# The feed-forward down projection as seven half-size products, with weight sums made by accumulating DMAs

## The chip, the core and the metric

The kernel runs on one core of a Trainium2 chip. The metric is the device time of one execution in microseconds, as the median over runs. Five engines work side by side, each through its own instructions in order: TensorE (PE in the profile; its weight loads are PEld), VectorE (DVE), ScalarE (ACT), GpSimd (POOL) and SyncE (SP, which issues most DMAs). Accumulators of TensorE lie in PSUM, everything else on the chip in SBUF.

## What is computed

A stack of mixing layers over 512 tokens of 1024 features: a first block (sparse attention and gated linear attention), a gated feed-forward layer, then four further attention layers. All is float32. Only the feed-forward layer is changed:

```
h = rmsnorm(x, norm_ffn)
g = silu(h @ w_ffn_gate) * (h @ w_ffn_up)      # 512 x 2816
x = x + g @ w_ffn_down                         # 2816 x 1024
x = rmsnorm(x, norm_final)
```

## The kernel before

**Precision.** A float32 matrix is kept as two halves of a faster format: the high part is made by ScalarE (line 214) and the low part by VectorE (line 215). A product takes three matmuls, high by high, low by high and high by low (`mm3`, lines 273 to 276). A weight piece is a raw tile `wr` (pool of 3, loaded by SP through `wload`), and its halves `wh` and `wl` (pool of 6). Ah and Al are the halves of the activations.

**Feed-forward.** The 2816 hidden features are 22 chunks of 128. They are computed in pairs of chunks: `pair` makes the gate product of a pair by `halves_product` (already seven products of halves, matmuls of 256 columns, with weight sums made on VectorE), the up product plainly (`proj_feat`, 512 columns), then tanh on ScalarE, sums and products on VectorE, and the split of the result into the tiles `hdh` and `hdl`. The first four chunks are computed plainly, and `half_sums` prepares token sums for the rest. The halves of silu are folded in as a factor 0.5 later.

**Down.** After 8, 8 and 6 chunks `down` multiplies what is there with the matching rows of w_ffn_down through `out_proj`: for each half of the 1024 columns and each of four row blocks of 128 tokens, n chunks times three matmuls of 512 columns into one PSUM tile of the pool `pj` (three tiles; `s` and `t` have two, `o` one). The epilogue adds it to the residual:

```
nc.vector.scalar_tensor_tensor(out=xv, in0=ps, scalar=0.5, in1=xv, op0=ALU.mult, op1=ALU.add)
```

In the last part the epilogue also takes squares (ScalarE), the norm (`rms_scale` on POOL, then line 1038 on VectorE with the row `gf`, which POOL loads by `broadcast_row`) and transposes the block for the next layer (`to_feat`, line 372).

**Order.** The instructions of each engine are put in order once, when the kernel is built, by a scheduler with its own estimate of durations. The chip follows that order: an engine that waits at one instruction holds back all behind it.

Of the kernel before, what the change touches and what calls it, by code (L numbers as in the profile page):

```python
# [10 lines left out]
F32 = mybir.dt.float32  # L11
# [7 lines left out]
S = 512  # L19
# [13 lines left out]
FF_PARTS = (8, 8, 6)  # L33
# [94 lines left out]
class Net:  # L128
# [99 lines left out]
    def wload(self, w, k0, kc, *ranges, pool=None):  # L228

        n = sum(r[1] for r in ranges)  # L230
        t = (self.wraw if pool is None else pool).tile([128, 1024], F32, name="wr")
# [654 lines left out]
    def half_sums(self, pool, room):  # L886

        nc = self.nc
        lo, hi, t0, t1 = slice(0, 4), slice(4, 8), slice(0, 256), slice(256, 512)
        q = lambda t, k, tok: t[:, k, tok]  # L890
        f11, f21, f12, f22 = (room.tile([128, 4, 256], F32, name=n) for n in ("f11", "f21", "f12", "f22"))
        for f, k, tok in ((f11, lo, t0), (f22, hi, t1), (f21, lo, t1), (f12, hi, t0)):
            nc.vector.tensor_tensor(out=f, in0=q(self.Ah, k, tok).bitcast(F32), in1=q(self.Al, k, tok).bitcast(F32), op=ALU.add)
        nc.vector.tensor_tensor(out=f22, in0=f21, in1=f22, op=ALU.add)
        nc.vector.tensor_tensor(out=f21, in0=f11, in1=f21, op=ALU.subtract)
        nc.vector.tensor_tensor(out=f11, in0=f22, in1=f11, op=ALU.subtract)
        nc.vector.tensor_tensor(out=f12, in0=f12, in1=f11, op=ALU.subtract)
        out = {"a11": (q(self.Ah, lo, t0), q(self.Al, lo, t0)), "a12": (q(self.Ah, hi, t0), q(self.Al, hi, t0)), "a22": (q(self.Ah, hi, t1), q(self.Al, hi, t1))}

        def splits():  # L900
            for n, src in (("s2", f11), ("s3", f21), ("s1", f22), ("s4", f12)):
                h, l = (pool.tile([128, 4, 256], F32R, name=n + u) for u in "hl")
                self.split_into(h, l, src)
                out[n] = (h, l)
            return out

        return splits

    def halves_product(self, pool, raws, sums, w, n0, out):
# [5 lines left out]
        v1 = self.wload(w, 0, KD, (n0 + 128, 128), pool=raws)  # L915
# [47 lines left out]
    def ffn(self):  # L963
        nc, a, tc = self.nc, self.a, self.tc
        with ExitStack() as c1:
            f1 = c1.enter_context(tc.tile_pool(name="f1", bufs=1))
            raws = c1.enter_context(tc.tile_pool(name="fr", bufs=1))
            most = max(FF_PARTS)
            hd = [f1.tile([128, most, S], F32R, name=n) for n in ("hdh", "hdl")]
            st = f1.tile([128, NB, 2], F32, name="fss")  # L970
            gf = f1.tile([128, D], F32, name="gf")
            self.broadcast_row(gf, a["norm_final"])
            wg, wu = a["w_ffn_gate"][0], a["w_ffn_up"][0]

            def hidden(m, s, u, tok=slice(0, S)):
# [4 lines left out]
            with tc.tile_pool(name="f0", bufs=1) as f0:  # L980
                for m in (0, 2):
                    wgs, wus = self.w_cols(wg, m * 128), self.w_cols(wu, m * 128)
                    for t in range(2):
                        halves = 1 if m or t else 2
                        for hf in range(halves):
# [5 lines left out]
                            s = f0.tile([128, S], F32, name="fg", bufs=2)[:, 0:n]  # L991
                            self.silu2(s, pg)
                            hidden(m + t, s, pu, tok)
                    if m == 0:
                        splits = self.half_sums(f1, f0)
                sums = splits()
            f2 = c1.enter_context(tc.tile_pool(name="f2", bufs=2))

            def pair(m, col):
# [466 lines left out]
```

## Time and profile before

| | |
|---|---|
| median of 3 runs | 1863.44 us (1862.99 to 1863.57) |
| the profiled execution | 1861.58 us |
| its span | 1859.8 us |
| TensorE busy | 1816.9 us, 98% |
| VectorE busy | 1216.1 us, 65% |
| ScalarE busy | 905.2 us, 49% |
| GpSimd busy | 155.6 us, 8% |

The span is the time from the first to the last instruction; the execution's own time has the start and end of the program in it too. Busy shares are of the span. Line numbers such as L1029 are those of the kernel printed above.

### The profile page before, as it was taken

The page shows a single profiled execution, that of the slowest core. Times are in us where ns is not written, and L with a number is a line of the kernel's source. Part 1 is how long each engine was busy: PE and PEld are TensorE (multiplying, and loading weights), DVE is VectorE, ACT ScalarE, POOL GpSimd, SP SyncE. Part 2 cuts the span into 40 slices and gives each one's busy share as a digit, 9 for nine tenths or more (in the row PEclk, how much of TensorE's full clock was granted, in tenths as well). Part 3 has the DMA queues.
Part 4 walks back from the last instruction along what each step waited for, and adds up shares of the span by engine and source line. Part 5 has one row for each costly group of instructions (what it writes and reads, how often), then busy time and mean ns, then how long its engine had stood idle before and what let it go on. Part 6 is the DMA issues. An engine that isn't in the chain of part 4 may idle for free.

```text
span 1859.8 us, 27291 instructions
## 1 busy us (share of the span) xinstructions
PE 1816.9 (98%) x10119; PEld 1494.7 (80%) x10119; DVE 1216.1 (65%) x3050; ACT 905.2 (49%) x2024; POOL 155.6 (8%) x213
## 2 busy tenths in 40 slices
PE   7999999999999999999999999999999999999997
PEld 6877787678888988889887798877888877988775
DVE  5554387754844664656878675576776666788866
ACT  4543236743432442445666444473565563366651
POOL 2211100000000000001000011242000000200001
PEclk9999999999999999999999999999999999999999
DMA  7222141042332442333221233211422222232111
GB/s 219 79 58 57 36 127 41 19 146 79 103 103 68 116 132 71 93 93 96 54 68 58 70 93 91 69 55 38 115 78 59 78 80 69 76 88 59 48 56 45
DMA packets 200751, 148.13 MB, mean 80 GB/s; under 512 B 8765, under 2 KB 178538, under 8 KB 200618
## 3 DMA queue, kind: packets, MB, share of 16 engines
q1 hardware_dynamic: 198826, 140.97, 26.5%
q0 software_dynamic: 1792, 5.42, 0.9%
q8 instruction: 79, 1.29, 0.3%
q14 instruction: 54, 0.44, 0.1%
HBM read 144.27 MB, written 2.10 MB: 79 GB/s over the span
## 4 chain that ended last, share of the span: by engine, by line
PE 91%; DVE 4%; ACT 2%; issue 2%; DMA 0%; POOL 0%; SPq 0%; POOLq 0%; DVEq 0%; ACTq 0%
PE pj L273 22%; PE pj L275 22%; PE pj L276 21%; PE o L350 4%; PE t L337 3%; PE pj L937 3%; PE s L937 1%; PE s L311 1%; PE o L273 1%; PE o L276 1%; PE s L275 1%; PE o L275 1%; PE s L273 1%; PE s L276 1%; DVE wl L215 1%
## 5 line engine op out<-in xcount | busy, mean ns | idle before, releaser
L214 ACT ACTIVATE wh<-wr 128x1024 fp32r<-128x1024 f32 (+9 forms) x406 | 294.6, 755 | 402.5 <-PE pj L275 158.0
L215 DVE TENSOR_TENSOR wl<-wr,wh 128x1024 fp32r<-128x1024 f32 (+9 forms) x406 | 338.3, 856 | 213.1 <-ACT wh L214 208.5
L273 PE MATMUL pj<-Ah,wh 128*128 128x512 f32 (+1 forms) x888 | 347.8, 392 | 2.2 <-DVE fg L288 0.9
L275 PE MATMUL pj<-Al,wh 128*128 128x512 f32 (+1 forms) x888 | 346.4, 390 | 0.2 <-DVE Al L215 0.2
L276 PE MATMUL pj<-Ah,wl 128*128 128x512 f32 (+1 forms) x888 | 345.6, 390 | 0.0
L273 PE MATMUL pj<-wh,Ah 128*128 128x512 f32 (+5 forms) x640 | 218.0, 341 | 4.7 <-ACT Ah L214 4.6
L275 PE MATMUL pj<-wl,Ah 128*128 128x512 f32 (+5 forms) x640 | 215.9, 337 | 0.0
L276 PE MATMUL pj<-wh,Al 128*128 128x512 f32 (+5 forms) x640 | 213.8, 338 | 2.1 <-DVE Al L215 2.0
L273 PEld LDWEIGHTS pj<-Ah,wh 128*128 128x128 f32 x888 | 167.3, 188 | 37.2 <-PE s L276 1.6
L276 PEld LDWEIGHTS pj<-Ah,wl 128*128 128x128 f32 x888 | 167.3, 188 | 35.0 <-issue 1.5
L275 PEld LDWEIGHTS pj<-Al,wh 128*128 128x128 f32 x888 | 167.3, 188 | 33.0 <-issue 0.8
L327 ACT ACTIVATE sp<-sp,nm 128x128 f32<-128x128 f32 (+3 forms) x256 | 142.9, 559 | 75.5 <-DVE nm L326 73.4
L205 ACT ACTIVATE pt<-t 128x512 f32<-128x512 f32 (+3 forms) x288 | 115.2, 445 | 105.9 <-PE t L337 66.6
L324 DVE CUSTOM_DVE_ANT_0 sp<-s,c_causal 128x128 f32<-128x128 f32 (+3 forms) x256 | 121.2, 487 | 56.5 <-PE s L276 23.5
L273 PEld LDWEIGHTS pj<-wh,Ah 128*128 128x128 f32 x640 | 120.6, 188 | 19.6 <-ACT Ah L214 7.3
L276 PEld LDWEIGHTS pj<-wh,Al 128*128 128x128 f32 x640 | 120.2, 188 | 14.1 <-DVE Al L215 3.1
L275 PEld LDWEIGHTS pj<-wl,Ah 128*128 128x128 f32 x640 | 120.7, 189 | 10.9 <-issue 0.2
L337 PE MATMUL t<-ident,sp 128*128 128x128 f32 x640 | 108.9, 278 | 5.1 <-ACT pt L205 5.0
L337 PEld LDWEIGHTS t<-ident,sp 128*128 128x128 f32 x640 | 77.3, 140 | 30.8 <-ACT pt L205 12.8
L331 DVE TENSOR_SCALAR sp<-sp,rc 128x128 f32<-128x128 f32 (+3 forms) x256 | 96.8, 383 | 5.0
L273 PE MATMUL pj<-wh,hdh 128*128 128x512 f32 x176 | 68.5, 390 | 0.3 <-DVE X L1029 0.3
L275 PE MATMUL pj<-wl,hdh 128*128 128x512 f32 x176 | 68.6, 390 | 0.0
(480 smaller groups left out, 3375.1 us busy)
## 6 DMA issues: line engine op xcount, KB each, us to landing
wr<-in_w_in_dram SPq DMA_DIRECT2D x34, 512.0 KB, 3.9
wr<-in_fox_w_in_dram SPq DMA_DIRECT2D x30, 512.0 KB, 4.1
wr<-in_w_ffn_gate_dram SPq DMA_DIRECT2D x22, 512.0 KB, 3.9
wr<-in_w_ffn_up_dram SPq DMA_DIRECT2D x22, 512.0 KB
wr<-in_w_ffn_down_dram SPq DMA_DIRECT2D x22, 512.0 KB, 3.8
wr<-in_swa_w_in_dram SPq DMA_DIRECT2D x20, 512.0 KB, 3.9
wr<-in_mla_w_in_dram SPq DMA_DIRECT2D x16, 512.0 KB, 3.9
wr<-in_mla_w_out_dram SPq DMA_DIRECT2D x16, 512.0 KB, 3.7
```

Source lines behind the costliest of these rows:

```text
L205: return self.nc.scalar.activation(out, in_, AF.Copy, scale=1.0 if scale is None else scale)
L214: self.nc.scalar.activation(h, src, AF.Copy)
L215: self.nc.vector.tensor_tensor(out=l, in0=src, in1=h.bitcast(F32), op=ALU.subtract)
L273: mm = self.nc.tensor.matmul(ps, lhsT=ah, rhs=bh, start=i == 0, stop=False)
L275: self.nc.tensor.matmul(ps, lhsT=ah, rhs=bl, start=False, stop=False)
L276: mm = self.nc.tensor.matmul(ps, lhsT=al, rhs=bh, start=False, stop=i == n - 1)
L324: nc.vector.tensor_tensor_reduce(out=v, in0=ps, in1=self.causal[:, S - n:S], scale=1.0, scalar=LOWEST, op0=ALU.add, op1=ALU.max, accum_out ...
L327: nc.scalar.activation(v, v, AF.Exp, bias=nm[:, g], accum_out=sm[:, g])
L331: nc.vector.tensor_scalar(v, v, rc[:, g], None, ALU.mult)
L337: nc.tensor.transpose(ps[:, (b - j) * 128:(b - j + 1) * 128], sp[:, POFF[b] + j * 128:POFF[b] + j * 128 + 128], self.ident)
L350: mm = self.nc.tensor.matmul(po[64 * i:64 * i + 64, j * 128:S], lhsT=value(j, i), rhs=pt[:, TOFF[j]:TOFF[j] + (NB - j) * 128], start=first ...
L937: nc.tensor.matmul(ps, lhsT=x, rhs=y, start=first and k == 0 and i == 0, stop=last and k == 3 and i == 2, skip_group_check=True)
```

## The change

The parts are now 6, 6, 6 and 4 chunks. With the chunks of a part taken as even and odd ones, tokens as two halves and columns as two halves, the down product is a two by two product of blocks, and it is made with seven products instead of eight. Each pair's hidden features are therefore combined into seven operands (`even`, `odd`), split into the tiles `hdh` and `hdl`, which now hold seven sets of 256 tokens. The weight sums are not made by an engine: a raw quarter of the weights is loaded into the tile x, split, and then the next quarter is added to it in place by a DMA that accumulates, issued by POOL; x receives three such additions, y one. Every product is added, with its sign, to the places of X that need it. The token sums (`half_sums`) are made in two pieces, and gf is loaded in the last part, into a tile that x used.

```diff
-FF_PARTS = (8, 8, 6)
+FF_PARTS = (6, 6, 6, 4)
...
+            def even(j, s, u):
                 nc.vector.tensor_tensor(out=s, in0=s, in1=u, op=ALU.mult)
-                self.split_into(hd[0][:, m, tok], hd[1][:, m, tok], s)
+                nc.vector.tensor_tensor(out=s[:, T1], in0=s[:, T0], in1=s[:, T1], op=ALU.subtract)
+                operands(j, 0, s)
+
+            def odd(j, pool, s, t, u):
+                nc.vector.tensor_tensor(out=t, in0=t, in1=u, op=ALU.mult)
+                e, f = (pool.tile([128, S], F32, name="fu", bufs=2) for _ in range(2))
+                nc.vector.scalar_tensor_tensor(out=e[:, T1], in0=s[:, T1], scalar=-1.0, in1=t[:, T1], op0=ALU.mult, op1=ALU.subtract)
+                nc.vector.tensor_tensor(out=e[:, T0], in0=e[:, T1], in1=s[:, T0], op=ALU.add)
+                operands(j, 4, e)
+                nc.vector.tensor_tensor(out=f[:, T0], in0=e[:, T1], in1=t[:, T0], op=ALU.add)
+                operands(j, 6, f[:, T0])
+                operands(j, 2, t)
...
+                def add(t, h, o):
+                    for v, (r, rc) in zip(t, pieces):
+                        nc.gpsimd.dma_start(v, quarter(r, rc, h, o), accum_op=ALU.add)
...
+                def update(ps, b, half, sign):
                     xv = self.X[:, b, half * 512:half * 512 + 512]
-                    nc.vector.scalar_tensor_tensor(out=xv, in0=ps, scalar=0.5, in1=xv, op0=ALU.mult, op1=ALU.add)
+                    nc.vector.scalar_tensor_tensor(out=xv, in0=ps, scalar=0.5 * sign, in1=xv, op0=ALU.mult, op1=ALU.add)
...
-                self.out_proj(a["w_ffn_down"][0], Split([(0, n, *hd)]), epilogue, kc=n, k0=k0)
+                x = raw(0, 0, raws.tile([128, 1536], F32, name="wr"))
+                w = weights(x)
+                pa = [self.pj(), self.pj()]
+                for i in range(2):
+                    product(pa[i], 0, w, i, first=True)
+                    update(pa[i], i, 0, 1)
+                add(x, 1, 0)
+                w = weights(x)
+                pc = [self.pss(), self.pss()]
+                for i in range(2):
+                    product(pc[i], 4, w, i, first=True)
+                    update(pc[i], 2 + i, 1, 1)
+                add(x, 1, 1)
+                w = weights(x)
+                for i in range(2):
+                    product(pa[i], 5, w, i)
+                    update(pa[i], i, 1, -1)
+                y = raw(1, 1)
+                w = weights(y)
+                for i in range(2):
+                    product(pc[i], 6, w, i, last=True)
+                    update(pc[i], i, 1, 1)
+                    squares(i, 1)
+                add(y, 1, 0)
+                w = weights(y)
+                for i in range(2):
+                    product(pa[i], 1, w, i)
+                    update(pa[i], 2 + i, 1, -1)
+                    squares(2 + i, 1)
+                w = weights(raw(0, 1))
+                add(x, 0, 1)
+                w4 = weights(x)
...
+                pb = [self.pst(), self.pst()]
+                for i in range(2):
+                    product(pb[i], 2, w, i, first=True, last=True)
+                    update(pb[i], i, 0, 1)
+                    squares(i, 0)
+                    norm(i)
+                for i in range(2):
+                    product(pa[i], 3, w4, i, last=True)
+                    update(pa[i], 2 + i, 0, 1)
+                    squares(2 + i, 0)
+                    norm(2 + i)
```

How the order of the instructions moves is shown at three places. A row has the line, the operation, the tile written and the tiles read, the shape, and the semaphores waited for: DMAHW is a DMA that SP issued, DMASW one that POOL issued, PE, DVE, Activation and Pool the engines.

ScalarE before, the last pair of the second part: fg_5948 and fg_5949 are its two gate results, fu its tanh, hdh its operands, the wh tiles weights.

```order
L214 ACTIVATE wh_6275<-wr_6273 128x1024 [waits DMAHW6_49,PE_49]
L214 ACTIVATE wh_6281<-wr_6279 128x1024 [waits DMAHW7_49,PE_49]
L205 ACTIVATE fg_5948<-pj_5974 128x256 [waits PE_49]
L1020 ACTIVATE fu_6109<-fg_5948 128x512 [waits Activation_49]
L1020 ACTIVATE fu_6112<-fg_5949 128x512 [waits DVE_49]
L214 ACTIVATE hdh_4339<-fg_5948 128x512 [waits DVE_49]
L214 ACTIVATE hdh_4339<-fg_5949 128x512 [waits DVE_49]
```

ScalarE after, the last pair of the second part: fg_5584 and fg_5585 are its gate results; wr_5791 is x of this down, wr_5886 and wr_5887 are y.

```order
L214 ACTIVATE wh_5858<-wr_5791 128x1024 [waits DMASW4_49,PE_49]
L205 ACTIVATE fg_5584<-pj_5610 128x256 [waits PE_49]
L1059 ACTIVATE fu_5745<-fg_5584 128x512 [waits DVE_49,Activation_49]
L1059 ACTIVATE fu_5748<-fg_5585 128x512 [waits DVE_49]
L214 ACTIVATE wh_5862<-wr_5791 128x512 [waits DMASW5_49]
L214 ACTIVATE wh_5890<-wr_5886 128x1024 [waits DMAHW7_49,PE_49]
L214 ACTIVATE wh_5894<-wr_5887 128x512 [waits DMAHW2_49,PE_49]
L214 ACTIVATE hdh_4339<-fg_5585 128x512 [waits DVE_49]
L214 ACTIVATE hdh_4339<-fg_5584 128x512 [waits DVE_49]
L214 ACTIVATE hdh_4339<-fu_5780 128x512 [waits DVE_49]
```

Where the operand splits followed the tanh directly, four weight splits now stand among them: one of an x sum ahead of the copy, and one of an x sum and two of y between tanh and operands.

TensorE after, the same pair: from the end of the last product of its gate (pj_5610, 17 rows above the first row here) on, 20 matmuls of the down need nothing of this pair; the last of them and what follows are shown.

```order
L1100 MATMUL pj_5803<-wh_5794,hdl_4340 128x512
L1100 MATMUL pj_5803<-wh_5794,hdh_4339 128x512
L1100 MATMUL pj_5803<-wl_5795,hdh_4339 128x512
L1100 MATMUL pj_5803<-wh_5794,hdl_4340 128x512
L1100 MATMUL pj_5802<-wh_5798,hdh_4339 128x512 [waits Activation_49]
L1100 MATMUL pj_5802<-wl_5799,hdh_4339 128x512
L1100 MATMUL pj_5803<-wh_5798,hdh_4339 128x512
L1100 MATMUL pj_5803<-wl_5799,hdh_4339 128x512
L1100 MATMUL pj_5802<-wh_5798,hdl_4340 128x512 [waits DVE_49]
L1100 MATMUL pj_5803<-wh_5798,hdl_4340 128x512
L1100 MATMUL s_5834<-wh_5830,hdh_4339 128x512 [waits Activation_49]
```

The first matmul that waits for ScalarE here is the first that needs operands of the last pair; in the kernel before, rows of that kind stood behind matmuls for several row blocks.

ScalarE after, the last pair of the last part: fg_7061 and fg_7062 are its gate results, wr_7268 is x, wr_7330 is y, wr_7377 the fourth raw quarter.

```order
L205 ACTIVATE fg_7061<-pj_7087 128x256 [waits PE_49]
L1059 ACTIVATE fu_7222<-fg_7061 128x512 [waits DVE_49,Activation_49]
L1059 ACTIVATE fu_7225<-fg_7062 128x512 [waits DVE_49]
L214 ACTIVATE wh_7355<-wr_7330 128x1024 [waits DMASW5_49]
L214 ACTIVATE wh_7379<-wr_7377 128x1024 [waits DMAHW1_49]
L214 ACTIVATE hdh_4339<-fg_7062 128x512 [waits DVE_49]
L214 ACTIVATE hdh_4339<-fg_7061 128x512 [waits DVE_49]
```

GpSimd after, the same part: three accumulating DMAs into x, one into y, and the load of gf.

```order
L1085 DMA wr_7268<-in_w_ffn_down_dram 128x2x512 [waits DMAHW0_49,DMAHW2_49,DMASW7_49,DMAHW4_49,DMASW6_49,DVE_49]
L1085 DMA wr_7268<-in_w_ffn_down_dram 128x2x512 [waits DMASW2_49,DVE_49]
L1085 DMA wr_7268<-in_w_ffn_down_dram 128x2x512 [waits DMASW3_49,DVE_49]
L1085 DMA wr_7330<-in_w_ffn_down_dram 128x2x512 [waits DMAHW3_49,DMAHW7_49,DMASW1_49,DVE_49]
L222 DMA wr_7388<-in_norm_final_dram 128x1024 [waits DMASW4_49,DVE_49]
```

The split of the y sum, wh_7355, waits for the fourth of these DMAs and stands ahead of the split of wr_7377 and of the operands of the last pair.

VectorE before, the end of the block: the last four updates (L1029), norms (L1038) and splits of transposed blocks (Al).

```order
L1029 SCALAR_TENSOR_TENSOR X_86<-pj_7116,X_86 128x512 [waits PE_49]
L1036 TENSOR_TENSOR ss1_7138<-fss_4341 128x1 [waits Activation_49]
L1038 SCALAR_TENSOR_TENSOR X_86<-X_86,rmso_7142,gf_4342 128x1024 [waits DMASW2_49,DVE_49,Pool_49]
L1029 SCALAR_TENSOR_TENSOR X_86<-pj_7159,X_86 128x512 [waits PE_49]
L1036 TENSOR_TENSOR ss1_7181<-fss_4341 128x1 [waits Activation_49]
L1038 SCALAR_TENSOR_TENSOR X_86<-X_86,rmso_7185,gf_4342 128x1024 [waits DVE_49,Pool_49]
L1029 SCALAR_TENSOR_TENSOR X_86<-pj_7202,X_86 128x512 [waits PE_49]
L215 TENSOR_TENSOR Al_88<-t_7145,Ah_87 128x4x128 [waits Activation_49]
L1036 TENSOR_TENSOR ss1_7224<-fss_4341 128x1 [waits Activation_49]
L215 TENSOR_TENSOR Al_88<-t_7152,Ah_87 128x4x128 [waits Activation_49]
L1038 SCALAR_TENSOR_TENSOR X_86<-X_86,rmso_7228,gf_4342 128x1024 [waits DVE_49,Pool_49]
```

VectorE after, the end of the block: updates (L1104), sums of squares (L1114), norms (L1116).

```order
L1104 SCALAR_TENSOR_TENSOR X_86<-pj_7275,X_86 128x512 [waits PE_49]
L1116 SCALAR_TENSOR_TENSOR X_86<-X_86,rmso_7405,wr_7388 128x1024 [waits DMASW6_49,DVE_49,Pool_49]
L215 TENSOR_TENSOR wl_7695<-wr_7692,wh_7694 128x864 [waits DMAHW6_49,Activation_49]
L215 TENSOR_TENSOR Al_88<-t_7408,Ah_87 128x4x128 [waits Activation_49]
L215 TENSOR_TENSOR Al_88<-t_7415,Ah_87 128x4x128 [waits Activation_49]
L1104 SCALAR_TENSOR_TENSOR X_86<-t_7391,X_86 128x512 [waits PE_49]
L215 TENSOR_TENSOR wl_7701<-wr_7698,wh_7700 128x864 [waits DMAHW7_49,Activation_49]
L1114 TENSOR_TENSOR ss1_7431<-fss_4341 128x1 [waits Activation_49]
L1114 TENSOR_TENSOR ss1_7461<-fss_4341 128x1 [waits Activation_49]
L1114 TENSOR_TENSOR ss1_7491<-fss_4341 128x1 [waits Activation_49]
L1238 MEMSET scale_7520 128x2 [waits DVE_49]
L1116 SCALAR_TENSOR_TENSOR X_86<-X_86,rmso_7435,wr_7388 128x1024 [waits Pool_49]
```

The updates of the four row blocks were spread over the matmuls of the last column half, each followed by its norm; now the last updates of three row blocks are made behind the last products, and the norms of three blocks come together.

## Rows read from the trace of the kernel before

**Rows 1.** The page's first part: busy time, share of the span, instructions.

```profile
span 1859.8 us, 27291 instructions
...
PE 1816.9 (98%) x10119; PEld 1494.7 (80%) x10119; DVE 1216.1 (65%) x3050; ACT 905.2 (49%) x2024; POOL 155.6 (8%) x213
```

**Rows 2.** Busy time by stretch, feed-forward block; then granted clock, DMA share, GB/s.

```profile
core 0: us, PE busy (x) PEld busy (x) DVE busy (x) ACT busy (x) POOL busy (x), PEclk, DMA share, GB/s
...
425.00:845.00 420.00, 417.85 (x2276) 361.59 (x2275) 238.61 (x308) 152.28 (x231) 8.06 (x21) 1.00 0.32 95
```

**Rows 3.** What TensorE waits for, 425 to 845: total us, times, longest.

```profile
PE pj L273 <- DVE fg L288: 0.9, 1, 0.9
...
PE pj L273 <- DVE X L1029: 0.3, 1, 0.3
```

**Rows 4.** Timeline of TensorE, four places: start, us, line, operation.

```profile
429.79 0.39 PE L273 MATMUL pj<-wh,mgh 128*128 128x512 f32 x1
...
431.42 0.40 PE L275 MATMUL pj<-wl,mgh 128*128 128x512 f32 x1
...
689.01 0.28 PE L937 MATMUL s<-s4h,wh 128*128 128x256 f32 x1
...
690.29 0.28 PE L937 MATMUL s<-s4h,wl 128*128 128x256 f32 x1
...
691.36 0.40 PE L273 MATMUL pj<-wh,hdh 128*128 128x512 f32 x1
...
699.33 0.39 PE L276 MATMUL pj<-wh,hdl 128*128 128x512 f32 x1
```

**Rows 5.** Groups by form, 425 to 845: count, busy us, mean ns, idle before.

```profile
L215 DVE TENSOR_TENSOR wl<-wr,wh 128x1024 fp32r<-128x1024 f32 x78 | 94.2, 1223 | 54.9 <-ACT wh L214 54.1
...
L275 PE MATMUL pj<-wl,hdh 128*128 128x512 f32 x176 | 68.6, 390 | 0.0
...
L1029 DVE SCALAR_TENSOR_TENSOR X<-pj,X 128x512 f32<-128x512 f32 x24 | 16.4, 689 | 42.4 <-PE pj L276 42.2
```

**Rows 6.** Timeline of VectorE, tail of the last pair before a down.

```profile
690.61 0.42 DVE L1008 TENSOR_TENSOR fg<-part,s 128x256 f32<-128x256 f32 x1 [1.61 <-PE s L937]
691.59 2.36 DVE L215 TENSOR_TENSOR wl<-wr,wh 128x1024 fp32r<-128x1024 f32 x2 [0.56 <-ACT wh L214]
693.87 1.28 DVE L1021 SCALAR_TENSOR_TENSOR fg<-fu,fg 128x512 f32<-128x512 f32 x2
...
696.45 1.29 DVE L215 TENSOR_TENSOR hdl<-fg,hdh 128x512 fp32r<-128x512 f32 x2
702.93 0.69 DVE L1029 SCALAR_TENSOR_TENSOR X<-pj,X 128x512 f32<-128x512 f32 x1 [5.19 <-PE pj L276]
```

**Rows 7.** Timeline of ScalarE, the same tail.

```profile
690.49 2.01 ACT L214 ACTIVATE wh<-wr 128x1024 fp32r<-128x1024 f32 x2 [2.75 <-PE s L937]
692.41 0.36 ACT L205 ACTIVATE fg<-pj 128x256 f32<-128x256 f32 x1
692.80 1.15 ACT L1020 ACTIVATE fu<-fg 128x512 f32<-128x512 f32 x2
695.78 1.23 ACT L214 ACTIVATE hdh<-fg 128x512 fp32r<-128x512 f32 x2 [1.83 <-DVE fg L976]
```

**Rows 8.** Timeline of VectorE, end of the block: norms of the last two row blocks.

```profile
828.47 1.28 DVE L1038 SCALAR_TENSOR_TENSOR X<-X,rmso,gf 128x1024 f32<-128x1024 f32 x1
...
834.78 1.29 DVE L1038 SCALAR_TENSOR_TENSOR X<-X,rmso,gf 128x1024 f32<-128x1024 f32 x1 [0.35 <-POOL rmso L225]
```

**Rows 9.** DMA queues and issues: packets, MB, share; KB, median us to landing.

```profile
q0 software_dynamic: 1792, 5.42, 0.9%
...
og<-in_ln_g_dram POOLq DMA_DIRECT2D x4, 512.0 KB, 3.9
...
gf<-in_norm_final_dram POOLq DMA_DIRECT2D x1, 512.0 KB, 5.3
```

**Rows 10.** Busy time around the issue of gf's load (478.8).

```profile
474.00:503.00 29.00, 27.60 (x159) 23.70 (x158) 28.25 (x36) 11.85 (x18) 1.34 (x3) 1.00 0.38 109
```

More of the change, by code (lines that the diff above doesn't have):

```diff
@@ L890, in half_sums @@
         q = lambda t, k, tok: t[:, k, tok]
[L891 to L895, printed above, removed]
@@ L909, in halves_product @@
+        return out, steps()
     def halves_product(self, pool, raws, sums, w, n0, out):
@@ L990, in ffn, with pair @@
                             self.proj_feat(pu, wus[t], self.act, tok=tok)
[L991 to L996, printed above, removed]
+                            self.silu2(s[:, tok], pg)
+                            if halves == 2:
+                                nc.vector.tensor_tensor(out=s[:, tok], in0=s[:, tok], in1=pu, op=ALU.mult)
+                        g.append(s)
+                        if t == 0 and halves == 2:
+                            nc.vector.tensor_tensor(out=s[:, T1], in0=s[:, T0], in1=s[:, T1], op=ALU.subtract)
+                            operands(0, 0, s)
+                        elif t == 0:
+                            even(m // 2, s, pu)
+                            next(steps)
+                        else:
+                            odd(m // 2, f0, g[0], s, pu)
+                            if m == 0:
+                                next(steps)
             f2 = c1.enter_context(tc.tile_pool(name="f2", bufs=2))
-            def pair(m, col):
-                g = [f2.tile([128, S], F32, name="fg", bufs=4) for _ in range(2)]
+            def pair(j, col):
+                g = [f2.tile([128, S], F32, name="fg", bufs=3) for _ in range(2)]
                 def out(t, half, x, y):
@@ new lines, in add, with weights, product @@
+                def add(t, h, o):
+                    for v, (r, rc) in zip(t, pieces):
+                        nc.gpsimd.dma_start(v, quarter(r, rc, h, o), accum_op=ALU.add)
+                def weights(t):
+                    parts = []
+                    for v, (r, rc) in zip(t, pieces):
+                        h, l = self.wtile(rc, 512)
+                        self.split_into(h, l, v)
+                        parts.append((r, rc, h, l))
+                    return Split(parts)
+                def product(ps, q, w, i, first=False, last=False):
+                    tok = slice(q * 256 + i * 128, q * 256 + i * 128 + 128)
+                    for j in range(nk):
+                        (ah, al), (bh, bl) = (o[:, j, tok] for o in ops), w.at(j, slice(0, 512))
+                        for u, (x, y) in enumerate(((ah, bh), (ah, bl), (al, bh))):
+                            nc.tensor.matmul(ps, lhsT=x, rhs=y, start=first and j == 0 and u == 0, stop=last and j == nk - 1 and u == 2, skip_group_check=True)
@@ L1035, in epilogue, with norm @@
+                def norm(b):
+                    if final:
                         ss = self.sm(1, "ss1")
```

84 lines of the change are left out of this document (57 added, 27 removed).

## Prediction

> **What bounds the kernel now.** I read the page's first part first: TensorE is busy for 98% of the span and VectorE for 65% [rows 1]. Then I cut out the stretch that the change touches, the feed-forward block from about 425 to 845 us. There TensorE is busy 417.85 of 420 us at a granted clock of 1.00, VectorE 238.61, ScalarE 152.28 [rows 2], and the list of what TensorE waits for in it has no entry above 0.9 us [rows 3]. So here time is the number of matmul columns, and a matmul less is time less. The reverse holds too: nothing is idle into which a new TensorE wait could fall, so every microsecond that TensorE is made to wait is lost.
>
> The timeline gives the pace. 35 steps of 512-column matmuls take 699.33 − 691.36 = 7.97 us, 0.228 each; seven steps elsewhere take 431.42 − 429.79 = 1.63, 0.233. I take 0.23. Eleven steps of 256 columns take 1.28, 0.117 each [rows 4]. The mean of 390 ns in the grouped view [rows 5] is the length of one in the pipeline, not its price.
>
> **What is removed.** The down projection has 3 × 176 = 528 matmuls of 512 columns [rows 5]. After: seven products of two token halves, with 3 terms for each of nk chunk pairs: 42 nk, and nk is 3, 3, 3 and 2, so 462. 66 × 0.23 = **−15.2 us**. That is all the change can give.
>
> **What is added on VectorE and ScalarE.** By the groups [rows 5], weight splits (22 of 1024 columns at 1.22 us become seven sets of 1024 + 512 in three parts, seven of 1024 in the last): 48.6 instead of 26.9, +21.8. X updates 56 instead of 24, at 0.69: +22.1. Per pair one more 512-column and one 256-column low split and four 256-column sums; taking a 256-column one at 0.42, as VectorE's sum at 690.61 [rows 6], that is 2.8 us × 11 = +30.7. The half sums in two pieces: about +1.8. VectorE goes to about 315 of 405 us, ScalarE to some 183. On average both fit beside TensorE, and VectorE now idles 1.6 to 5.2 us at a stretch around a pair [rows 6], so I cost this at nothing between the downs. Inside a down with nk = 3 the 126 matmuls last 29.0 us and hide VectorE's own 7 × (1.22 + 0.69) + 14 × 0.69 = 23.1; without that cover it would be about 23 us per part.
>
> **What the downs lose.** The engines run in order, so what counts is what stands ahead of what.
>
> *Pair tail, parts two and three.* Before, the tail of a part's last pair (copy of the gate product at 692.41, tanh, two products each, split) ends at 697.74, 5.3 us [rows 6, 7], while TensorE, never waiting, works through down matmuls that don't need this pair; the first accumulator that does is finished only at 702.93 [rows 6], 10.5 us after that copy began. After, 20 matmuls lie between the last gate product and the first that needs the pair's operands (front: PE order): 4.6 us. And ScalarE has the weight splits wh_5890 and wh_5894 ahead of the operand splits; wh_5894 needs the buffer that the last of those 20 matmuls reads. So from 4.6 us on: 0.63 for it, 0.60 and 0.63 for two operand splits (1.23 for a pair [rows 7]), a handover of about 0.1: TensorE waits **1.9**. Its next waits are for the third operand set (about 0.5), the X update that frees the accumulator (0.5), a late update before the fourth product (0.3), and the weight split of the next pair (0.5): **3.7 per part, 7.4** for two. None depends on the accumulating DMA while it lands within 6 us.
>
> *Pair tail, first part.* Here ScalarE splits wh_5016 and wh_5020 between copy and tanh, and VectorE two low splits (1.2 and 0.6) ahead of the up product. Copy 0.36 + 0.95 + 0.6 + 0.6 + tanh 0.6, then 0.68 + 0.60 + 1.14 + 0.60 + 0.60 + 0.42 on VectorE and 0.63 on ScalarE make 7.8, with some eight handovers at 0.05 to 0.1 about 8.4. Cover: 12 × 0.117 + 12 × 0.23 = 4.2. So 4.2, and 1.3 for the operand splits behind: **5.5**.
>
> *Last part.* wh_7355 waits for an accumulate on the y weights that is queued fourth on POOL's queue (issue order: three on x, then y) and only after the low split wl_7333; it stands ahead of wh_7379, which TensorE needs after 60 matmuls of 512 and 60 of 256 columns from the end of the product t_7088: 20.9 us. The chain from that same point: 2.9 us of VectorE up to wl_7271, an accumulate L, 2.3 for a split pair (1.06 + 1.22), L, 2.3, 1.15 for wl_7333, L, 2.0 for the two ScalarE splits, some 0.7 of handovers. That is 3L + 11.4, so TensorE waits **3L − 9.5**. Three further small waits for late operands and updates: **3.0**.
>
> *End of the block.* Before, the four row blocks finish one after another: squares, norm and transpose of one lie beside the next one's matmuls, and the norms are 6 us apart (828.47, 834.78) [rows 8]; TensorE waits 0.3 us for an update in all [rows 3]. After, blocks one, two and three get their last update behind the last matmuls. The first transpose waits for an update and a norm, 0.69 + 1.29 + handover, 2.15; the transposes of the second block and their split another 1.0 + 2.4, two more 0.3 each: **6.0**.
>
> *L.* No accumulating DMA runs in the kernel before, and the software queue carried 5.42 MB in all [rows 9]. Nearest rows: four loads of 512 KB that POOL issues late in the kernel land after 3.9 us in the median, that of gf, issued while VectorE was busy for 28.25 of 29 us, after 5.3 [rows 9, 10]. A down is such a stretch, and an accumulate must also read what it adds to. I take 5.3; bounds 3.9 and, if the read-back costs a whole second transfer, 10.6. The Trainium skill ("DMA: Bandwidth & Descriptors", Anatomy of one DMA — SWDGE (gpsimd) path) fits a software-queue DMA as 2.0 us plus bytes over 436 GB/s, an estimated 3.2 us here; by it the last part's wait would be 0.1 and the time about 1870. The rows above show no 512 KB landing that short.
>
> **Sum.** −15.2 + 7.4 + 5.5 + (3 × 5.3 − 9.5 = 6.4) + 3.0 + 6.0 = +13.1. The profiled execution took 1861.58 us with a span of 1859.8 [rows 1], 0.1% under the median of 1863.44; I add to the median: **1876.5**. With L = 3.9 the sum is +8.9 less 0.3 in the first part, 1872; with 10.6 the last part gives 22.3, parts two and three about 2 us more per us above 6 (+18) and the first about 1 per us (+5): 1916.
>
> **Rivals.**
> *Faster, the tails are shorter than I step them.* Place: ScalarE's queue in the four pair tails. I add each wait in series; several may run beside one another, and buffers may come free earlier. If a tail costs only what it exceeds its cover by (0.4 to 1 us, say 0.7) and the end only the first norm, 2.2, with L = 3.9: 2.8 + 2.2 + 2.2 = 7.2, so −8.0: 1855.5. It decides once all new waits are under 15.2 us. For it: VectorE idles before and after such stretches [rows 6]. Against: the order is fixed at build time and shows the weight splits ahead.
> *About the same:* waits of 12 to 19 us, half of mine: 1860 to 1867.
> *The accumulate is slow.* POOL must issue 28 of these while VectorE is busy nearly throughout; the one load of 512 KB of this kind lands latest (5.3 against 3.9) [rows 9, 10]. With L at 8 to 10.6 the order blocks ScalarE for whole transfers: 1893 to 1916. The Trainium skill ("SBUF — State Buffer", Who interferes with whom) has GpSimd starved of descriptor writing when VectorE holds the shared port in its two-port modes. The busy 29 us were nearly all two-operand subtractions and sums, for which that page infers no such block; by it L would stay near 3.9.
> *VectorE becomes the bound.* In a down it has 23.1 us of its own, some 5 of the last tail and 7 of the next pair's splits: 35 against 29. Were none of it moved into idle stretches, 3 × 6 us come on top: 1895. Against it: those idle stretches, and the 315 of 405.
>
> **How the numbers follow.** A measurement here tells about 0.2%, 3.7 us. Forecast (L 3.9 to 6.5, waits as stepped, 1868 to 1885): 0.48. Slow accumulate or VectorE-bound (1885 to 1916): 0.22. Same: 0.10. Faster (1848 to 1860): 0.20. Leaving out about one in ten on each side: 1855 to 1900. For the forecast alone 1868 to 1885.
>
> **What would show it.** Down matmuls 3 × 154 at 0.23 us apart. In TensorE's waits: operand high splits on ScalarE, X updates on VectorE, together 25 to 31 us between about 540 and 850. Accumulating DMAs landing in about 5 us. TensorE idle 5 to 8 us once, just before the last part's P2 product, with ScalarE's wh split waiting for a DMA. A gap of about 2 us at the first transpose after the block. The forecast is wrong if those waits are under 15 us in all, or if VectorE rather than a DMA or ScalarE's order is named for most of them; a granted clock below 1.00 behind a long wait would add time that I haven't counted.

## The result: 1.6% slower, and the profile after

The changed kernel takes 1893.36 us (median of 4 runs, 1888.77 to 1896.05) against 1863.51 us for the kernel before on the same chip: a ratio of 1.0162 with a 95% interval of 1.0149 to 1.0174, or +29.9 us. I forecast +13.1.

The page's first part, after (its span is 1894.3 us):

```profile
PE 1820.4 (96%) x10053; PEld 1491.6 (79%) x10053; DVE 1279.5 (68%) x3186; ACT 933.0 (49%) x2076; POOL 187.3 (10%) x241
```

TensorE has the 66 matmuls less that the change promised (10119 in [rows 1]), and yet is busy for 3.5 us longer. So some of its matmuls took more time each. VectorE has 63 us more and ScalarE 28, somewhat less than I had worked out.

What TensorE waits for in the block, 425 to 900 us (total, times, longest). L1100 is a matmul of the seven products, L372 a transpose for the next layer, L1116 a norm, L1047 a sum of the gate product; hdh and hdl are operands, wh weights:

```profile
PE pj L1100 <- ACT hdh L214: 10.8, 4, 6.9
PE t L1100 <- ACT wh L214: 7.6, 1, 7.6
PE s L1100 <- DVE fg L1047: 2.9, 1, 2.9
PE t L372 <- DVE Al L215: 2.7, 2, 2.3
PE pj L1100 <- DVE hdl L215: 2.4, 2, 1.2
PE t L372 <- DVE X L1116: 2.3, 1, 2.3
```

These six make 28.7 us, where [rows 3] had nothing above 0.9. The places are the forecast ones: operands of a last pair, the weights ahead of the last part's P2 (the 7.6), the transposes behind the block.

The granted clock isn't in that list. Windows over the block and over the microseconds behind the waits (columns as in [rows 2]):

```profile
425.00:900.00 475.00, 444.34 (x2365) 380.44 (x2364) 318.65 (x505) 193.98 (x327) 46.01 (x61) 0.96 0.44 107
...
548.00:552.00 4.00, 0.00 (x0) 0.00 (x0) 3.88 (x7) 2.62 (x4) 2.09 (x2) 0.76 0.46 62
552.00:556.00 4.00, 1.80 (x4) 1.49 (x5) 3.97 (x9) 2.09 (x4) 2.14 (x2) 0.50 1.06 175
556.00:560.00 4.00, 4.00 (x11) 3.02 (x10) 2.12 (x5) 1.10 (x2) 0.00 (x0) 0.50 0.87 156
560.00:564.00 4.00, 4.00 (x19) 3.27 (x18) 3.26 (x5) 1.04 (x2) 0.00 (x0) 0.96 0.21 53
652.00:656.00 4.00, 2.77 (x7) 1.66 (x6) 3.78 (x8) 0.94 (x2) 1.79 (x2) 0.56 1.05 166
656.00:660.00 4.00, 4.00 (x12) 3.18 (x11) 1.84 (x3) 1.06 (x1) 0.00 (x0) 0.59 0.66 117
752.00:756.00 4.00, 3.90 (x9) 2.83 (x10) 2.94 (x7) 0.94 (x2) 0.34 (x1) 0.50 1.03 155
756.00:760.00 4.00, 4.00 (x15) 3.15 (x14) 1.83 (x3) 1.69 (x2) 0.00 (x0) 0.71 0.29 52
832.00:836.00 4.00, 2.17 (x4) 1.45 (x5) 3.38 (x5) 2.58 (x4) 0.00 (x0) 0.50 0.20 54
836.00:840.00 4.00, 4.00 (x11) 3.05 (x10) 2.83 (x7) 1.32 (x3) 0.00 (x0) 0.50 0.46 142
...
864.00:868.00 4.00, 1.48 (x8) 0.93 (x7) 3.55 (x5) 1.00 (x2) 2.06 (x2) 0.94 0.09 34
868.00:872.00 4.00, 4.00 (x20) 3.97 (x18) 0.69 (x1) 0.60 (x1) 0.00 (x0) 0.63 0.00 0
```

Before, the clock was 1.00 over the whole block [rows 2]. Here it falls while TensorE stands (0.76 in 548 to 552, without a matmul) and is at 0.50, the 1.2 GHz level, or little above for the work that follows. I count as lost in a window its busy time times one minus the clock: 1.80 × 0.50 + 4.00 × 0.50 + 4.00 × 0.04 = 3.1 us behind the first part's wait, then 2.9, 3.1, 3.1 and 1.6: **13.7 us** in all. The four runs say the same: mean clocks of 0.988 and 0.987 go with 1896 us, 0.991 and 0.992 with 1889 to 1891. The profiled run is the longest of them.

The timeline of TensorE shows it matmul by matmul, at the first part's last pair, the second's, and the last part's (start, duration, operation, idle time ahead):

```profile
554.20 0.80 PE L1100 MATMUL pj<-wh,hdh 128*128 128x512 f32 x1 [6.89 <-ACT hdh L214]
...
556.07 0.63 PE L1100 MATMUL s<-wh,hdh 128*128 128x512 f32 x1
556.50 0.63 PE L1100 MATMUL s<-wl,hdh 128*128 128x512 f32 x1
...
560.33 0.40 PE L1100 MATMUL pj<-wh,hdl 128*128 128x512 f32 x1
560.56 0.40 PE L1100 MATMUL pj<-wh,hdh 128*128 128x512 f32 x1
...
651.13 0.50 PE L1100 MATMUL pj<-wh,hdh 128*128 128x512 f32 x1 [1.89 <-ACT hdh L214]
...
653.56 1.22 PE L1100 MATMUL pj<-wh,hdl 128*128 128x512 f32 x2 [1.24 <-DVE hdl L215]
...
655.58 0.63 PE L1100 MATMUL s<-wh,hdh 128*128 128x512 f32 x1
656.00 0.63 PE L1100 MATMUL s<-wl,hdh 128*128 128x512 f32 x1
...
824.32 0.51 PE L1100 MATMUL s<-wh,hdh 128*128 128x512 f32 x1 [2.94 <-DVE fg L1047]
824.66 0.40 PE L1100 MATMUL s<-wl,hdh 128*128 128x512 f32 x1
824.89 0.40 PE L1100 MATMUL s<-wh,hdl 128*128 128x512 f32 x1
```

The steps are 0.43 us from 556.07 to 556.50 and again 0.23 from 560.33 on.

The accumulating DMAs. The chain of the last part is seen on GpSimd (the issues) and, after three rows of the first part, on ScalarE (the splits that wait for what lands):

```profile
806.08 1.20 POOL L1085 DMA_DIRECT2D wr<-in_w_ffn_down_dram  x1 [53.75 <-DVE wl L215]
...
823.10 1.20 POOL L1085 DMA_DIRECT2D wr<-in_w_ffn_down_dram  x1 [7.32 <-DVE wl L215]
824.64 1.22 POOL L1085 DMA_DIRECT2D wr<-in_w_ffn_down_dram  x1 [0.34 <-DVE fg L1047]
```

```profile
545.69 1.06 ACT L214 ACTIVATE wh<-wr 128x1024 fp32r<-128x1024 f32 x1 [2.14 <-DMA wr<-in_w_ffn_down_dram]
546.66 0.61 ACT L1059 ACTIVATE fu<-fg 128x512 f32<-128x512 f32 x1
548.07 0.63 ACT L214 ACTIVATE wh<-wr 128x512 fp32r<-128x512 f32 x1 [0.80 <-DMA wr<-in_w_ffn_down_dram]
...
811.96 1.06 ACT L214 ACTIVATE wh<-wr 128x1024 fp32r<-128x1024 f32 x1 [2.98 <-DMA wr<-in_w_ffn_down_dram]
...
831.53 2.00 ACT L214 ACTIVATE wh<-wr 128x1024 fp32r<-128x1024 f32 x2 [6.61 <-DMA wr<-in_w_ffn_down_dram]
833.44 1.13 ACT L214 ACTIVATE hdh<-fg 128x512 fp32r<-128x512 f32 x2
```

From issue to split it is 811.96 − 806.08 = 5.9 us and, with two in the queue, 831.53 − 824.64 = 6.9. For those last 6.61 us ScalarE can't split the operands queued behind it. The issues of 500 to 900 us (KB, median us to landing) put it beside plain loads by SP:

```profile
wr<-in_w_ffn_down_dram POOLq DMA_DIRECT2D x16, 512.0 KB, 5.9
...
wr<-in_w_ffn_down_dram SPq DMA_DIRECT2D x12, 512.0 KB, 4.5
```

### The profile page after: what moved, and what is told of

Same layout as the page of the kernel before. It is cut to its first block, busy times and chain, and to the rows that moved or that the text cites. A ratio compares the mean times of both kernels' runs of the same rounds, so it can differ in the third digit from the quotient of the medians.

```text
span 1894.3 us, 27488 instructions
## 1 busy us (share of the span) xinstructions
PE 1820.4 (96%) x10053; PEld 1491.6 (79%) x10053; DVE 1279.5 (68%) x3186; ACT 933.0 (49%) x2076; POOL 187.3 (10%) x241
## 4 chain that ended last, share of the span: by engine, by line
PE 83%; DVE 5%; issue 3%; DMA 3%; ACT 3%; POOL 1%; SPq 0%; POOLq 0%; DVEq 0%; ACTq 0%
PE pj L273 19%; PE pj L275 19%; PE pj L276 18%; PE o L350 4%; PE t L337 3%; PE pj L1100 3%; DMA wr<-in_w_ffn_down_dram 3%; PE pj L948 2%; DVE wl L215 1%; PE s L1100 1%; ACT wh L214 1%; PE s L311 1%; PE s L275 1%; PE s L948 1%; PE s L273 1%
## 5 line engine op out<-in xcount | busy, mean ns | idle before, releaser
L214 ACT ACTIVATE wh<-wr 128x1024 fp32r<-128x1024 f32 (+9 forms) x433 | 312.9, 753 | 411.9 <-PE pj L275 153.5
L215 DVE TENSOR_TENSOR wl<-wr,wh 128x1024 fp32r<-128x1024 f32 (+9 forms) x433 | 356.6, 847 | 217.6 <-ACT wh L214 199.3
L275 PEld LDWEIGHTS pj<-Al,wh 128*128 128x128 f32 x888 | 167.2, 188 | 33.3 <-issue 0.8
L214 ACT ACTIVATE Ah<-t 128x512 fp32r<-128x512 f32 x48 | 27.0, 596 | 73.5 <-PE t L372 63.4
L1085 POOL DMA_DIRECT2D wr<-in_w_ffn_down_dram x28 | 30.2, 1115 | 317.6 <-DVE wl L215 297.0
```

The lines of the kernel that those rows point to most:

```text
L214: self.nc.scalar.activation(h, src, AF.Copy)
L215: self.nc.vector.tensor_tensor(out=l, in0=src, in1=h.bitcast(F32), op=ALU.subtract)
L275: self.nc.tensor.matmul(ps, lhsT=ah, rhs=bl, start=False, stop=False)
```

## The experiments

The theory after the result: in-order queues hold operands up behind weights, the weights behind accumulating DMAs, and each group of waits costs a low clock on top. Rivals: VectorE is the bound; the parts of 6, 6, 6 and 4 cost it; the order of the queues alone does; the accumulates alone do. Each ratio is against runs of the kernel before on the same chip, in three rounds. In kernels with added lines the lines are shifted: L1107, L1106 or L1103 stands for L1100, L1110 for the update L1104, L373 and L1123 for L372 and L1116.

### 1. The sums as plain loads

```diff
-                        nc.gpsimd.dma_start(v, quarter(r, rc, h, o), accum_op=ALU.add)
+                        nc.sync.dma_start(v, quarter(r, rc, h, o))
```

> The 28 accumulating DMAs become plain loads of the same quarters into the same places, issued by SyncE; this leaves the additions of weights out, all else stays in order. Theory (the order of ScalarE's and VectorE's queues makes the waits; only the last part's three transfers in series depend on the landing time): the landing falls from 5.9 to about 4 us, the last part's long wait shrinks by 3 x 1.9 plus about 1 for the two additions that now queue behind each other, the first part's by about 1.5; the other waits and the stretches at the low clock stay: 1883 to 1887 us, TensorE still waits over 18 us in the block. Rival (accumulating DMAs as such are the cause): nearly all new waits go, 1865 or less.

Measured 1877.66 us, 1.0082 [1.0067, 1.0097]. That is 15 us less than with accumulates, more than I expected. Issues and TensorE's waits, 500 to 900 and 425 to 900 us:

```profile
wr<-in_w_ffn_down_dram SPq DMA_DIRECT2D x28, 512.0 KB, 3.7
```

```profile
PE pj L1100 <- ACT hdh L214: 8.0, 4, 4.0
PE t L1100 <- ACT wh L214: 3.1, 1, 3.1
```

The landing falls from 5.9 to 3.7 us, the last part's wait from 7.6 to 3.1, and the first part's, which I had thought nearly free of the DMA, from 6.9 to 4.0. But 8 us of operand waits stay. Not only the landing changed, though: the scheduler built other orders too. In each of the first three parts ScalarE has one weight split earlier than in the changed kernel; in the first part the split at 540.74 now stands ahead of the gate product's copy at 541.71, where the copy (543.16) stood ahead of the split (545.69). So the 15 us are those of both together.

### 2. The last part plain

The last part's `pair` and down are those of the kernel before.

```diff
...
-                        pair(m // 2, (k0 + m) * 128)
-                down(part, k0, n)
+                        pair(m // 2, (k0 + m) * 128, part == len(FF_PARTS) - 1)
+                if part == len(FF_PARTS) - 1:
+                    down_plain(k0, n)
+                else:
+                    down(part, k0, n)
```

> The last part of four chunks is done plainly as before (8 instead of 7 products, no weight sums, updates and norms spread over the row blocks); parts one to three stay as changed. Theory: the 12 us of waits and 2.5 us of low clock ahead of the last part's products and the 8.5 us of waits and about 1.2 of low clock at the end of the block go, 12 matmuls more cost 2.7: about 1872 (1869 to 1876). Rival (VectorE's added work is the bound, spread over all parts): the last part has about a seventh of it, so 1885 to 1890.

Measured 1877.84 us, 1.0081 [1.0066, 1.0096]: about half of the loss lies in the last part and the end of the block. It fell by less than expected.

### 3. Fewer updates

```diff
                     product(pa[i], 0, w, i, first=True)
-                    update(pa[i], i, 0, 1)
...
                     product(pc[i], 4, w, i, first=True)
-                    update(pc[i], 2 + i, 1, 1)
...
                     product(pa[i], 5, w, i)
-                    update(pa[i], i, 1, -1)
```

> The readings of the accumulators into X after the products P0, P4 and P5 are left out (6 of 14 updates per part, 24 in all, 16.6 us of VectorE); their contributions are left out of the result. Theory: only the waits of TensorE for those readings and the work queued behind them go, 0.5 to 1 us per part: 1889 to 1892. Rival (VectorE is the bound in the downs): most of 16.6 us is won, 1880 or less.

Measured 1890.63 us, 1.0155 [1.0138, 1.0172], and the two largest waits stayed at 10.7 and 7.6 us. Some 16 us less of VectorE's work (24 updates at 0.69) gave 1.3 us by the ratios, which is within their intervals: VectorE's throughput isn't the bound.

### 4. The kernel before with the new parts

```diff
-FF_PARTS = (8, 8, 6)
+FF_PARTS = (6, 6, 6, 4)
```

> The kernel before with the parts 6, 6, 6 and 4 in place of 8, 8 and 6, and nothing else of the change. Theory: 528 down matmuls as before, eight more updates of X hidden under them: 1863 to 1866. Rival (a smaller part leaves too few matmuls that don't need its last pair, so the parts alone make the waits): 1870 or more, with TensorE waiting for operands of the last pair in each down.

Measured 1873.35 us, 1.0060 [1.0045, 1.0075]. The theory fell here: I had costed the parts at almost nothing, and by themselves, with eight products and no accumulate, they cost 10.4 us. Its waits hold one row that the changed kernel has word for word:

```profile
PE t L372 <- DVE Al L215: 2.7, 2, 2.3
```

In the order 6, 6, 4, 6 (expected as follows) it is 1869.42 us, 1.0035 [1.0022, 1.0048], between the theory and the rival.

> The kernel before with parts 6, 6, 4 and 6 (against 1863 with 8, 8, 6 and 1873 with 6, 6, 6, 4). Theory (a last part of 4 chunks leaves 12 matmuls per row block, too few for a block's norm, transpose and split, and a down of 4 too few for its last pair): most of the 10 us goes with a last part of 6: 1863 to 1867. Rival (a fourth part costs by itself): 1870 or more.

There that row is 0.4 us. So the long wait at the transposes, and the low clock behind it, belong to a last part of 4 chunks; the seven products aren't needed for it.

### 5. TensorE kept busy through the waits

Matmuls whose result nobody reads (28, 7 and 7 in the first three parts) stand ahead of the one that waits for the last pair.

```diff
+                    fill = [nc.tensor.matmul(spare, lhsT=self.Ah[:, 0, 0:128], rhs=self.Ah[:, 0], start=True, stop=True).ins for _ in range(idle)]
+                    self.after(fill[0], mms[4, 1, nk - 2, 2].ins)
...
+                    self.after(mms[0, 0, nk - 1, 0].ins, fill[-1])
```

> The changed kernel with matmuls of no use (28 of 512 columns in the first part, 7 in each of the next two, into a spare accumulator that nobody reads) put into TensorE's order right ahead of the first matmul that waits for the operands of the last pair; ScalarE's, GpSimd's and SyncE's orders stay. They take 6.4 and 1.6 us of a wait of 6.9 and 1.9. Theory (the granted clock falls because TensorE stood still, and the slow stretch behind each wait is a cost of its own): the wait is as long but filled, the stretches at the low clock behind it go in the first part and shrink in the next two, 3 to 7 us are won: 1886 to 1890. Rival (the low clock comes from somewhere else, or the operands also come later): 1893 or more.

Measured 1887.93 us, 1.0148 [1.0132, 1.0165], as expected. The wait for operand splits, and the windows that hold the three tails:

```profile
PE pj L1103 <- ACT hdh L215: 1.0, 4, 0.5
```

```profile
535.00:606.00 71.00, 70.43 (x387) 60.22 (x386) 51.92 (x75) 30.37 (x45) 6.32 (x6) 1.00 0.53 126
606.00:673.00 67.00, 65.54 (x346) 55.24 (x345) 48.92 (x75) 27.01 (x42) 8.45 (x8) 1.00 0.52 114
...
735.00:795.00 60.00, 57.25 (x305) 48.09 (x305) 43.64 (x61) 25.57 (x36) 5.14 (x5) 1.00 0.52 124
```

The 42 matmuls (9.7 us at 0.23) take the place of 9.8 us of waits, and the clock stays at 1.00 where it was at 0.50. The profiled run reaches the end of the last part's last gate product 4.6 us sooner, counted from a matmul at the start of the block (433.55 to 821.09 us in the changed kernel, 430.87 to 813.83 here). The whole kernel is 3.5 us faster by the medians (29.9 and 26.4 us above the kernel before on the same chip) and 2.6 by the ratios, whose intervals overlap: that it is faster as a whole isn't clear of noise. That the low clock comes from TensorE's standing still is shown by the windows.

### 6. Operands ahead of weights

Every weight split from P5 on is put behind the splits of the last pair's operands, on ScalarE and VectorE.

```diff
+                        two = self.split_into(h, l, v)
+                        if late:
+                            for q in (0, 2, 4, 6):
+                                for now, then in zip(two, made[nk - 1, q]):
+                                    self.after(now, then)
...
```

> The changed kernel, with the weight splits for P5 and all later products ordered behind the operand splits of the part's last pair on ScalarE and VectorE; nothing else. Theory (what stands ahead in these two queues makes the waits): the first part's tail falls from 7 to about 1 us of wait, the last part's long wait from 7.6 to 2 or 3, some of it comes back when P5's weights are late, with less time at the low clock: 1870 to 1882. Rival (the accumulating DMA's landing is what is waited for, whoever stands where): the waits move to P5's weights and the time stays over 1887.

Measured 1910.81 us, 1.0262 [1.0246, 1.0277], slower still: the theory of the order alone fell. TensorE's waits:

```profile
PE pj L1107 <- ACT wh L214: 17.2, 6, 4.9
PE t L373 <- DVE X L1123: 7.1, 1, 7.1
...
PE pj L1107 <- ACT hdh L214: 3.5, 3, 1.6
```

The operand waits shrink from 10.8 to 3.5 us, and 17.2 us of waits for weights appear: the next accumulate can start only when the split of the last sum is done, and that now starts later. In the first part GpSimd's next issues move from 548.30 and 552.05 to 551.28 and 554.21, though this run began the block 2.1 us earlier, and ScalarE then stands:

```profile
562.82 1.06 ACT L214 ACTIVATE wh<-wr 128x1024 fp32r<-128x1024 f32 x1 [11.54 <-DMA wr<-in_w_ffn_down_dram]
```

The first norm is late as well (the 7.1).

### 7. More work ahead of the last pair

The pairs that are ready go first through P0, P2 and P4, with P2's weights loaded early, and the operand order of the last experiment.

```diff
+                for i in range(2):
+                    product(pa[i], 0, w, i, first=True, js=ready)
+                for i in range(2):
+                    product(pb[i], 2, w2, i, first=True, js=ready)
+                for i in range(2):
+                    product(pc[i], 4, wc, i, first=True, js=ready)
...
```

> As the run before, and P2, whose weights need no sum, is started together with P0 and P4: in each part the matmuls of these three that don't need the last pair come first, then the rest of the three. Theory (the change took away the cover of the pair tail): with 8 us of cover instead of 4.6 the tails of the first three parts cost 2 us or less each; the last part keeps 4 to 6, the end of the block about 6: 1858 to 1867. Rival (the chain of accumulating DMAs is too long for any order): over 1873.

Measured 1890.46 us, 1.0156 [1.0141, 1.0171], in the rival's range: no operand wait is left among the larger ones, but again waits for accumulated weights (11.5 and 5.5 us in two groups). With the last part plain and the parts 6, 6, 4 and 6:

> As the run before, with parts 6, 6, 4 and 6 of which the last is done plainly as in the kernel before: 48 matmuls less than before (11 us) and the end of the block as before. Theory: three tails of 1 to 4 us: 1855 to 1861. Rival as in the run before: over 1866.

Measured 1882.26 us, 1.0108 [1.0091, 1.0125], again in the rival's range.

### 8. P6 ahead of P5 as well

P6 and its sum for P1 start before P5, in the order of experiment 7 (the lines are those against it). With four parts in seven products, the last part then takes the squares of the first two row blocks ahead of P5's update, so the kernel leaves that update out of their norms:

```diff
-                w = weights(x)
-                for i in range(2):
-                    product(pa[i], 5, w, i)
-                    update(pa[i], i, 1, -1)
                 y = raw(1, 1)
...
                 add(y, 1, 0)
+                w = weights(x)
+                for i in range(2):
+                    product(pa[i], 5, w, i)
+                    update(pa[i], i, 1, -1)
```

> P2 first and operands first as in the run with 1890 us, and P6 ahead of P5, so that the y weights are split and added to 4 us earlier; parts 6, 6, 6 and 4. Theory: the waits for P1's weights (4.5, 2.8, 2.8 and 5.3 us with 1 to 2 us of low clock behind each) go or halve: 1872 to 1882. Rival (they move on to the x chain or to the next pair's weights): 1887 or more.

Measured 1884.55 us, 1.0116 [1.0101, 1.0131], between the theory and the rival. TensorE's waits for ScalarE's weight splits ahead of the down products fell to 1.1 us, but the next pair's gate weights, split behind them, now come late:

```profile
PE pj L949 <- ACT wh L214: 8.2, 2, 4.3
```

With the last part plain, parts 6, 6, 4 and 6:

> The same with parts 6, 6, 4 and 6, the last one plain as in the kernel before. Theory: from 1882 down by the waits for P1's weights, 15 us with the low clock: 1860 to 1870, level with the kernel before at best. Rival: 1878 or more.

Measured 1880.81 us, 1.0099 [1.0084, 1.0114], in the rival's range. Both miss what I expected of them.

### 9. No accumulating DMAs at all

```diff
                 def add(t, h, o):
-                    for v, (r, rc) in zip(t, pieces):
-                        nc.gpsimd.dma_start(v, quarter(r, rc, h, o), accum_op=ALU.add)
+                    return
```

In the changed kernel:

> The changed kernel without the 28 accumulating DMAs (the additions of weights are left out); every split and product stays. With 5.9 us of landing each the kernel takes 1893, with plain loads of 3.7 us in their place 1878. Theory as it stands now (the waits of the downs are the chain of transfers and splits in place, x - split - add - split - add, that no order of the queues shortens, plus what the part sizes cost by themselves): with no transfer in the chain the time goes down once more, to 1862 to 1870, and no wait above 3 us is left ahead of the down products. Rival (the order of the queues, as I first thought): the pair tails keep their 2 to 7 us and the time stays at 1873 to 1878.

Measured 1879.99 us, 1.0092 [1.0075, 1.0108]. Sums that cost nothing take off 13 us, no more than plain loads did, and 17 us of loss remain, with operand waits in the first three parts:

```profile
PE pj L1099 <- ACT hdh L214: 7.5, 3, 4.0
```

So the accumulates alone aren't the cause either. As in experiment 1 the scheduler also moved weight splits on ScalarE: one in each of the first three parts, and in the last part the two that stood between tanh and operands now stand ahead of the gate product's copy. The 13 us aren't those of the accumulates by themselves. The same edit in the order of experiment 8, with all parts in seven products and then with the last part plain:

> The version with P2 first, operands first and P6 ahead of P5 (1885 us with the additions), without the accumulating DMAs; parts 6, 6, 6 and 4. If the two causes together make the loss (the tails left without cover, and the chain of transfers in place, each hidden by the other when only one is cured): 1862 to 1872, against 1880 and 1885 with one of them cured. Rival (VectorE's and ScalarE's added work takes what is won, whatever the order): 1876 or more.

> The same with parts 6, 6, 4 and 6, the last one plain (1881 us with the additions), without the accumulating DMAs. Both causes together: 1856 to 1865, so level with the kernel before or a little under it, which would be the most that this down projection can give with free weight sums. Rival: 1872 or more.

Measured 1865.68 us, 1.0017 [1.0008, 1.0027], and 1862.93 us, 1.0003 [0.9994, 1.0013]. Waits and window of the former:

```profile
PE pj L1106 <- DVE X L1110: 6.5, 5, 4.3
PE s L1106 <- DVE X L1110: 1.9, 1, 1.9
```

```profile
478.00:860.00 382.00, 371.44 (x2037) 319.92 (x2037) 280.96 (x442) 167.35 (x278) 10.15 (x21) 0.99 0.30 88
```

Both came out as expected. By the ratios, order and accumulates together are worth 27.0 us (1.0162 − 1.0017, of 1863); the order alone is worth 8.6 (experiment 8) and the accumulates alone 13.0, so together 5 us more than their sum. With intervals of about 0.0015 to either side of each ratio, these 5 us are at the edge of what the runs can tell. In the order of experiment 8 ScalarE's queue stays as it was through the first three parts when the accumulates go, and there they are worth 18.4 us (1.0116 − 1.0017). That order does more than cover the pair tails: with P2 early, the first two row blocks no longer get their last update at the end, and the 2.7 us at the transposes are 0.4.

## Why the prediction was wrong in size

Direction and places held, and in the main the mechanism; the sum was 17 us short. By TensorE's timeline I took the distance between the starts of neighbouring matmuls, less the pace ([rows 4]), took off what the low clock lost, and got for each step:

| step of the prediction | forecast, us | waits, us | low clock, us |
|---|---|---|---|
| first part, last pair | 5.5 | 6.9 | 3.1 |
| second and third part | 7.4 | 6.8 | 6.0 |
| last part | 9.4 | 11.4 | 3.1 |
| end of the block | 6.0 | 8.2 | 1.6 |
| sum | 28.3 | 33.3 | 13.7 |

(The first part: 9.99 above the pace, less 3.06, is 6.9.) −15.2 + 33.3 + 13.7 = +31.8; the block takes 31 us longer in this profiled run. Its span is 34.5 us longer; of the rest, 2.4 us lie ahead of the block and 1.0 behind it, and no run says why.

- **Columns, −15.2:** right. 66 matmuls are gone, and the pace at full clock is still 0.23.
- **The step that failed: the sum of the waits had no term for the granted clock.** I named such a clock at the end as something not counted, though a new wait of 2 to 6 us stood in every part of my own sum. It made 13.7 us. Experiment 5 shows that the clock follows TensorE's standing still: with useless matmuls in the same places it stays at 1.00. The Trainium skill ("TensorE: Matmul & The Clock Gate", Part 1) lists 1.2 GHz as the level of an idle TensorE; the rows agree, with 0.50 in five of the windows above. It speaks against the change, and I should have weighed it.
- **First part, 5.5:** I put no DMA into this tail. ScalarE waited there 2.14 and 0.80 us for accumulated weights, each ahead of a tanh, and TensorE's first wait is 6.89 instead of 4.2. In experiment 1 it is 4.0.
- **Second and third part:** the first wait was forecast at 1.9 and is 1.89. The one for the third operands is 1.24 instead of 0.5; the others were smaller.
- **Last part, 3L − 9.5 + 3.0:** L was taken as 5.3 and is 5.9, and 6.9 where two stand in GpSimd's queue. With L of 5.9 the formula gives 8.2 for TensorE's idle time up to that product. It is 10.5: the weight wait of 7.6 and, ahead of it, one of 2.94 us for the gate product's sum, since VectorE too had weight splits of that chain ahead of it. By the estimate from the Trainium skill ("DMA: Bandwidth & Descriptors", SWDGE path) L would have been 3.2; the rows disagree.
- **End of the block, 6.0:** the two long waits came as stepped (2.3 us each, for the first norm and for VectorE's split of the second block); handovers around them, none above 1.1, make it 8.2. But the second comes with a last part of 4 chunks even in the kernel before (experiment 4), so the late updates that I named aren't needed for it.
- **VectorE costed at nothing between the downs:** right as to its throughput (experiment 3). The kernel of experiment 9 in the order of experiment 8 does all of the seven products' updates and splits, VectorE busy 281 of 382 us, and is 3 us from the kernel before. What is left there for TensorE to wait for is VectorE all the same, 8.4 us for updates.
- **The rival of a slow accumulate** had 1893 in its range, but with L of 8 to 10.6. At 5.9 it isn't that rival; that the time fell on its edge is chance.

Experiments 4, 6 and 9 say what the steps couldn't: the causes hang together. The weight sums form a serial chain in one tile (split, add, split), and operands and weights share two in-order queues, so curing the queue alone starves the chain (experiment 6) and curing the chain alone leaves the queue (experiment 9). With both cured, the 15.2 us of columns don't quite pay for the rest (1.0017): the smaller parts by themselves lose 7 to 10 us in the kernel before. Of these, the transposes' wait and its low clock are in the changed kernel too (experiment 4). How much of the others sits there wasn't separated, since the tiles for seven operands were only tried with parts of 6 and 4. That the remaining 3 us of experiment 9 are the updates that TensorE waits for (8.4, the longest 4.3 in the last part) is likely from its waits, but was not tried. None of these kernels beats the one before; the two nearest leave out the weight sums.

## What to carry to other kernels

Saved matmuls are worth their time only while TensorE stays fed: for each place where it will wait, add the wait and then the stretch at half clock behind it, here about 3 us for each part. List what stands ahead of the late operand in every in-order queue, and also what the chain behind that queue needs, before moving one ahead of the other; moving it may only change the name of the wait. Where two causes feed the same wait, test each alone and both together, since one alone can look harmful (experiment 6). And when the order is built anew for each edit, see whether the edit moved anything else in the queues (experiments 1 and 9).

## What the hardware showed that I had not expected

- An accumulating DMA of 512 KB into SBUF landed 5.9 us after its issue, a plain load of the same bytes by SP 3.7 (experiment 1), or 4.5 beside the accumulates; GpSimd was busy 1.20 us with each such issue.
- Whether the clock falls isn't told by the length of one wait: behind the 2.94 us at 824.32 the steps are back at 0.23 by 824.66 and TensorE waits again from 825.8 on, while behind 1.89 and 1.24 us at 651 to 654, with four matmuls between, they are 0.43.
- Useless matmuls in a wait kept the clock at 1.00 and brought TensorE to the last part 4.6 us sooner than the wait itself (experiment 5, one profiled run of each).
